# Group softmax on one core: GpSimdE instead of SyncE opens and closes the critical section and waits for the last two stores

## The chip, the cores and the metric

One core of a Trainium2 chip. The metric is the device time of one execution in microseconds (us). Durations of single instructions are in nanoseconds (ns). "The trace's records" are the start and duration of each single instruction in the trace; the views of the profile show them rounded to 0.1 us or summed up.

## The reference

```python
B, N, D, G = 4, 4096, 4352, 8          # x: float32, 285.2 MB; the output is as large
x_g = x.reshape(B, N, G, D // G)       # groups of 544 values
x_g = x_g - x_g.max(axis=-1, keepdims=True)
exp = np.exp(x_g)
out = exp / exp.sum(axis=-1, keepdims=True)
```

## The kernel before

The input is cut into 64 tiles of 128 partitions x 8704 values (4.4 MB), which pass through six buffers. SyncE issues the loads, VectorE takes each group's negative maximum, ScalarE the exponential with its sum, VectorE scales in place, and GpSimdE issues 62 of the 64 stores. SyncE issues the last two, since it has no loads left by then. The engines are ordered by semaphores alone, inside one critical section: one engine raises a flag that lets the others in, and at the end one engine raises a flag, collects the answers of the others, and all pass a final barrier.

```python
ctx.enter_context(tc.tile_critical(no_gpsimd_drain=True))   # SyncE opens and closes
...
for t in range(nt):                                          # SyncE: loads
    if t >= NT:
        nc.sync.wait_ge(stored[t % NT], 16 * (t // NT))
    ...
    nc.sync.dma_start(out=tile_in[:, :], in_=xt[t]).then_inc(landed[t % NT], 16)
    ...
for t in range(nt - LAST, nt):                               # SyncE: last two stores
    nc.sync.wait_ge(scaled, t + 1 if t < nt - 1 else len(parts))
    nc.sync.dma_start(out=ot[t], in_=bufs[t % NT][:, :]).then_inc(last_stored, 16)
nc.sync.wait_ge(last_stored, 16 * LAST)

for t in range(nt - LAST):                                   # GpSimdE: 62 stores
    nc.gpsimd.wait_ge(scaled, t + 1)
    nc.gpsimd.dma_start(out=ot[t], in_=bufs[t % NT][:, :]).then_inc(stored[t % NT], 16)
for t in range(nt - NT, nt - LAST):
    nc.gpsimd.wait_ge(stored[t % NT], 16 * (t // NT + 1))
nc.gpsimd.drain()
```

## Time and profile before

| | before |
|---|---|
| three runs | 1326.55, 1326.64, 1326.76 us |
| span of the profiled run | 1324.9 us |
| bytes moved | 570.5 MB at 431 GB/s over the span |
| first load issued | 0.960 us |
| sixteenth increment of the last store | 1323.532 us |
| from there to the end ("the tail") | 1.387 us |

The last three rows are from the trace's records. They cut the span in three: an opening without transfers, a stream of transfers that fills 99.8% of the time, and a tail without transfers. The lines of the profile that show it are in the prediction below.

### The profile page before, as it was taken

The numbers are of one execution on the slowest core, as the hardware profiler recorded it, in microseconds if no ns is written. First come the engines' busy times: TensorE is split into PE (matmuls) and PEld (weight loads), VectorE is DVE, ScalarE is ACT, GpSimd is POOL, SyncE is SP. The second block draws the span as 40 slices with busy tenths as digits, with TensorE's granted clock in tenths as the row PEclk, the third lists the DMA queues.
The fourth block names the chain that finished last, engine by engine and source line by source line (L and its number), as shares of the span: only waits on it lengthen the run. The fifth ranks groups of instructions, "written<-read, shape, count | busy, mean of one in ns | idle before, by whom it ended". The sixth has DMA issues, their size and how long they took to land.

```text
span 1324.9 us, 2463 instructions
## 1 busy us (share of the span) xinstructions
DVE 1190.0 (90%) x195; ACT 757.5 (57%) x2049; POOL 33.4 (3%) x66
## 2 busy tenths in 40 slices
DVE  5999999988989889898898998988989889898893
ACT  3765566547456465564655646556465474654751
POOL 0000000000000000000000000000000000000000
DMA  9999999999999999999999999999999999999998
GB/s 404 421 432 436 428 435 434 434 431 433 433 435 433 432 434 433 436 429 435 432 436 431 433 433 434 434 431 435 433 436 429 435 432 436 431 432 434 433 431 372
DMA packets 18582, 570.48 MB, mean 431 GB/s; under 512 B 2064, under 2 KB 2064, under 8 KB 2064
## 3 DMA queue, kind: packets, MB, share of 16 engines
q1 hardware_dynamic: 9648, 294.13, 51.5%
q0 software_dynamic: 8928, 276.30, 48.3%
q14 instruction: 6, 0.05, 0.0%
HBM read 285.21 MB, written 285.21 MB: 431 GB/s over the span
## 4 chain that ended last, share of the span: by engine, by line
another core or an unknown queue 69%; DVE 20%; DMA 7%; ACT 1%; SPq 1%; issue 0%
DVE xt L74 10%; DVE mx L61 10%; DMA out_dram<-xt 4%; DMA xt<-in_x_dram 4%; ACT xt L85 1%; SPq L104 1%; DVE rs L71 0%; SPq L166 0%; SPq L47 0%
## 5 line engine op out<-in xcount | busy, mean ns | idle before, releaser
L85 ACT ACTIVATE xt<-xt,mx 128x544 f32<-128x544 f32 x1024 | 750.2, 734 | 542.7 <-DVE mx L61 542.7
L61 DVE TENSOR_REDUCE mx<-xt 128x16 f32<-128x8704 f32 (+1 forms) x65 | 590.1, 9079 | 111.0 <-DMA xt<-in_x_dram 111.0
L74 DVE TENSOR_TENSOR xt<-xt,rs 128x8704 f32<-128x8704 f32 (+1 forms) x65 | 590.6, 9086 | 2.2
L85 ACT ACTIVATION_READ_ACCUMULATOR xt<-xt,mx 128x1 f32 x1024 | 191.8, 187 | 0.0
L118 POOL DMA_DIRECT2D out_dram<-xt x62 | 33.2, 535 | 1243.7 <-DVE xt L74 1243.7
L71 DVE RECIPROCAL rs<-sm 128x16 f32<-128x16 f32 (+1 forms) x65 | 15.7, 242 | 2.8 <-ACT xt L85 2.8
L123 ACT ACT_TABLE_LOAD x1 | 1.3, 1283 | 0.9 <-SPq L47 0.9
L155 POOL MEMSET const-float32-0.0<- 128x1 f32 x1 | 0.1, 99 | 0.2 <-issue 0.2
L155 POOL MEMSET const-bfloat16-1.0<- 128x1 bf16 x1 | 0.1, 102 | 0.0
L155 POOL MEMSET const-float32-1.0<- 128x1 f32 x1 | 0.1, 99 | 0.0
L155 POOL MEMSET const-uint8-127<- 128x1 uint8 x1 | 0.1, 99 | 0.0
## 6 DMA issues: line engine op xcount, KB each, us to landing
xt<-in_x_dram SPq DMA_DIRECT2D x63, 4352.0 KB, 33.1
out_dram<-xt POOLq DMA_DIRECT2D x62, 4352.0 KB, 50.6
out_dram<-xt SPq DMA_DIRECT2D x2, 4352.0 KB, 20.1
xt<-in_x_dram SPq DMA_DIRECT2D x2, 2176.0 KB, 36.0
```

The costliest lines, as they stand in the source:

```text
L61: i = nc.vector.reduce_max(out=mx[:, t % NT, g], in_=groups(t, g), axis=X, negate=True)
L71: nc.vector.reciprocal(out=rs[:, t % NT, g], in_=sm[:, t % NT, g]).wait_op(exp_done, n + 1, "sem-ge").then_inc(rec_done, 1)
L74: nc.vector.tensor_tensor(out=xg, in0=xg, in1=rs[:, t % NT, g].unsqueeze(2).to_broadcast([P, g.stop - g.start, Dg]), op=mybir.AluOpType.mu ...
L85: i = nc.scalar.activation(out=xg[:, g - gs.start, :], in_=xg[:, g - gs.start, :], func=Exp, bias=mx[:, t % NT, g:g + 1], scale=1.0, accum ...
L104: nc.sync.dma_start(out=tile_in[:, :], in_=xt[t]).then_inc(landed[t % NT], 16)
L118: nc.gpsimd.dma_start(out=ot[t], in_=bufs[t % NT][:, :]).then_inc(stored[t % NT], 16)
L123: nc.scalar.preload_act_table(Exp)
L155: nc = _bacc.Bacc("TRN2", target_bir_lowering=False, num_devices=1)
```

## The change

Its intent is to take one hand-over out of the two ends. GpSimdE releases the barrier at the start (at 0.646 us in the trace of the kernel before) and collects the one at the end (from 1324.168 us), so it may as well raise the section's flags, and SyncE can issue its first load without raising a flag first.

```diff
-    ctx.enter_context(tc.tile_critical(no_gpsimd_drain=True))
+    ctx.enter_context(tc.tile_critical(
+        sync_engine=mybir.EngineType.Pool, no_gpsimd_drain=True))
...
         nc.sync.dma_start(out=ot[t], in_=bufs[t % NT][:, :]).then_inc(last_stored, 16)
-    nc.sync.wait_ge(last_stored, 16 * LAST)
...
     nc.gpsimd.drain()
+    nc.gpsimd.wait_ge(last_stored, 16 * LAST)
```

## The prediction

What no trace or run of this case shows is cut from this text, and the cuts are marked. Where the text speaks of one DMA engine that ends behind the rest, what the trace has is one packet alone under way from 1321.769 to 1323.053 us, and the sixteenth increment 1.563 us after the fifteenth.

> **What bounds the kernel now.** I began with the head of the page, to see whether an engine is full.
>
> ```profile
> span 1324.9 us, 2463 instructions
> DVE 1190.0 (90%) x195; ACT 757.5 (57%) x2049; POOL 33.4 (3%) x66
> ...
> DMA  9999999999999999999999999999999999999998
> ...
> HBM read 285.21 MB, written 285.21 MB: 431 GB/s over the span
> ```
>
> VectorE is busy 90% of the time, but the DMA row is at nine tenths or more in 39 of 40 slices. Input and output are 4 x 4096 x 4352 values of four bytes, 285.2 MB each, so the 570.4 MB are what the problem demands, and at 431 GB/s they take 1324 us: the whole span. GpSimdE has 3% of work.
>
> Next the queue of SyncE, since the change takes duties from it.
>
> ```profile
> SPq L104 <- DMA out_dram<-xt: 1218.2, 58, 67.7
> SPq L112 <- DVE xt L74: 59.9, 2, 44.7
> ...
> SPq L155 <- PEq L155: 0.7, 1, 0.7
> SPq L166 <- SPq L166: 0.4, 1, 0.4
> SPq L166 <- PEq L166: 0.2, 1, 0.2
> ```
>
> Columns: microseconds waited in total, how many times, the longest. A load waits for the store that empties its buffer, 58 times, for 1218 us: one closed loop of transfers. The two lines that wait for VectorE are the final stores. All waits for other engines at the two ends of the program come to 0.7 + 0.4 + 0.2 us. That is the stuff the change rearranges.
>
> Then the stretches of the span, columns: length, busy time and instructions of each engine, clock, DMA share, GB/s.
>
> ```profile
> 1.00:100.00 99.00, 83.25 (x13) 57.52 (x154) 1.73 (x3) 1.00 0.99 422
> 100.00:1200.00 1100.00, 1008.15 (x164) 640.68 (x1736) 29.32 (x55) 1.00 1.00 433
> ...
> 1306.00:1323.60 17.60, 0.03 (x1) 0.00 (x0) 0.00 (x0) 1.00 0.81 350
> 1323.60:1324.90 1.30, 0.00 (x0) 0.00 (x0) 0.00 (x0) 1.00 0.00 0
> ```
>
> From 1.0 to 1323.6 us the transfers hold everything. Only the first 1.0 us and the last 1.3 us have no transfer in them. So 2.3 us, 0.17% of the span, is the most that any change to opening and closing could touch inside the span, and most of that stays.
>
> Last, what GpSimdE and SyncE do at the end, from the views of single lines (duration in ns, then start of the first and the last).
>
> ```profile
> L121 POOLq DRAIN  x1: 5129/5129/5129, 1312.1 to 1312.1; - x1
> ...
> L104 SPq COMPARE_BRANCH  x1: 33/33/33, 1323.5 to 1323.5; - x1
> ...
> L47 SPq EVENT_SEMAPHORE  x3: 17/17/28, 1323.7 to 1323.9; - x3
> ...
> L47 POOLq NOP  x1: 13/13/13, 1323.7 to 1323.7; - x1
> ```
>
> GpSimdE's own drain takes 5.13 us, but ends at 1312.08 + 5.13 = 1317.21 us. SyncE passes its wait for the last two stores only at 1323.55 us (the wait is carried by the branch that follows it). GpSimdE therefore stands idle for 6.3 us before the event that closes the section. This decides most of the question.
>
> [...] the last store's 16 increments come between 1320.31 and 1323.53 us, fifteen of them by 1321.97. Who waits for the sixteenth cannot make it come sooner. [...] The trace has 155 ns from SyncE's waiting branch at 1323.548, over one more branch, to its flag at 1323.703. [...] in the trace two successive semaphore instructions stand 78 ns apart on GpSimdE (1324.168 and 1324.246) and 64 to 70 ns on SyncE (1323.879, 1323.948, 1324.018, 1324.082), so they are close, with GpSimdE slightly slower.
>
> **The change, part by part.** I compared the two built programs, engine by engine. TensorE, VectorE and ScalarE keep every instruction; their flags merely come from GpSimdE. SyncE's loads and stores and GpSimdE's stores keep their order and waits. What moves is a handful of semaphore instructions: three fewer on SyncE, five more on GpSimdE.
>
> The opening. Before: GpSimdE leads the start barrier and releases it at 0.646 us; SyncE sees it (0.662), sets the section's flag (0.727, visible 0.743), and passes its own waiting branch at 0.803, 76 ns later than its flag instruction; the first load issues at 0.960, 157 ns after the branch. After: GpSimdE, which released the barrier with its instruction at 0.620, goes straight on to a branch and the flag, one step of 78 ns (estimate, from its spacing above): flag at about 0.70, visible at 0.72. SyncE, which no longer has a flag to set, reaches its branch where the flag instruction stood, about 0.727 to 0.74. The first load then issues about 157 ns later, at 0.89. Saved: 0.960 - 0.89 = 0.07 us. As the loads start a closed loop, this should move the whole schedule earlier by 0.07 us.
>
> The closing. Before, counted from the sixteenth increment at 1323.532: 16 ns to SyncE's branch, 155 ns to the flag (1323.703), then the answers of the others, three waits and a step, and SyncE's count into the final barrier at 1324.145; GpSimdE takes it up at 1324.168, 465 ns after the flag; from there to the end is 1324.919 - 1324.168 = 751 ns. After, GpSimdE has the same branch pair (16 + 155, estimate: same as SyncE). From its flag it needs: its own waiting no-op, 92 ns (SyncE's distance from flag to own answer, 1323.795 - 1323.703); two waits, a no-op and a branch with drain, 4 x 78 = 312; the drain's 34; and about 60 to the barrier's wait. Sum: 498 ns against 465, so 33 ns more. SyncE's chain runs beside it: its answer, two waits and two drains, one no-op fewer than before, about 465 - 64 = 401 ns. It hides behind the 498. The final barrier's 751 ns stay. Added: 0.03 us.
>
> GpSimdE's drain and its waits for older stores stay ahead of the new wait, and with 6.3 us of slack cost nothing. Sum: -0.07 + 0.03 = -0.04 us on 1326.64. I predict **1326.6 us**.
>
> **Rivals.** First, GpSimdE as closer is a slow one: if its drain and the wait ran one after the other, up to 5.1 us would be added, giving 1331.8 (0.4% slower). For it: the drain is the longest entry of all sequencer lines. Against it: the drain starts when an older store lands at 1311.97, not with the last one. It stays hidden unless that store lands over 6.3 us later.
>
> Second, the intended gain is real: SyncE saves a whole hand-over at the end because GpSimdE leads the final barrier. If the close collapsed to the barrier alone, the 613 ns from 1323.532 to SyncE's count at 1324.145 would shrink to perhaps 200, for 1326.2 us. Against it: SyncE still waits for all the answers before it enters the final barrier, so the trip is turned round rather than removed.
>
> Third, an early shift changes how loads and stores interleave. One of the 16 DMA engines ends 1.6 us behind the rest in the last store (1323.53 against 1321.97); an order that removed this would give 1325.0, and one that lengthened it by as much 1328.2. The loop's 58 waits, all of one kind, speak against a lasting effect of 0.07 us, yet this is the largest source of a difference over 0.2 us. [...]
>
> **Range and chances.** Three runs of before lie within 0.21 us (1326.55 to 1326.76), more than the effect I compute. The third rival sets the range: about two thirds of its 1.6 us either way gives 1325.5 to 1327.6. A change of 2% is 26.5 us, eleven times the 2.3 us without transfers, and neither drain nor stray engine reaches it. I give 0.99 to within 2%; the rest is for an effect on the stream of transfers that I do not see.
>
> **What would show it.** Right: first load issued at about 0.89 us; DMA share unchanged at 1.00 in the middle; the drain again about 5.1 us and over before the last store lands; GpSimdE's waiting branch within 20 ns of the last increment; 1.3 to 1.5 us from that increment to the end. Wrong: a drain that ends after the last store; a tail over 1.6 us or under 1.2; another spacing of the last store's increments; a middle that runs at another rate than 433 GB/s.

## The result, and the profile after

| | before | after |
|---|---|---|
| median, lowest to highest of 6 runs each | 1326.74 (1326.55 to 1327.48) | 1326.41 (1326.28 to 1326.50) |
| span of the profiled run | 1324.919 | 1324.654 |
| first load issued | 0.960 | 0.897 |
| first load to last increment | 1322.572 | 1322.368 |
| tail | 1.387 | 1.389 |

The ratio is 0.9997, with a 95% interval of 0.9984 to 1.001. Executions over 1.5% slower than the fastest of the same kernel are left out of the means.

The head of the page after the change:

```profile
span 1324.7 us, 2465 instructions
DVE 1190.0 (90%) x195; ACT 757.4 (57%) x2049; POOL 33.3 (3%) x66
...
HBM read 285.21 MB, written 285.21 MB: 431 GB/s over the span
```

There are two instructions more: the trace records six more on GpSimdE and four fewer on SyncE. Work and bandwidth are what they were. The waits of SyncE's queue after (total us, times, longest):

```profile
SPq L105 <- DMA out_dram<-xt: 1201.7, 57, 67.8
SPq L113 <- DVE xt L75: 59.1, 2, 43.9
SPq L108 <- DMA out_dram<-xt: 20.2, 1, 20.2
SPq L47 <- POOLq L47: 17.3, 1, 17.3
SPq L167 <- PEq L167: 0.8, 2, 0.5
SPq L156 <- PEq L156: 0.7, 1, 0.7
```

Against the lines before, the first group has lost one wait and 16.5 us (58 and 1218.2 before). This is not a gain: the lost wait was SyncE's for the last two stores, which stood in that group as it is carried by the branch of the same line (L104, at 1323.548 us). A wait of 17.3 us for GpSimdE's closing flag has come in its place. The wait moved, and it still ends when the last store lands.

The stretches after, cut where the transfers end (length, busy time and instructions of each engine, clock, DMA share, GB/s):

```profile
1.00:100.00 99.00, 83.31 (x13) 57.57 (x154) 1.73 (x3) 1.00 1.00 424
100.00:1200.00 1100.00, 1008.34 (x164) 640.58 (x1736) 29.23 (x55) 1.00 1.00 433
1306.00:1323.30 17.30, 0.00 (x0) 0.00 (x0) 0.00 (x0) 1.00 0.80 346
1323.30:1324.70 1.40, 0.00 (x0) 0.00 (x0) 0.00 (x0) 1.00 0.00 0
```

The middle runs at 433 GB/s as before, and 1.4 us without transfers remain at the end. The single lines at the close (durations in ns, then start of first and last):

```profile
L121 POOLq DRAIN  x1: 5129/5129/5129, 1311.8 to 1311.8; - x1
...
L105 POOLq COMPARE_BRANCH  x1: 33/33/33, 1323.3 to 1323.3; - x1
...
L47 POOLq EVENT_SEMAPHORE  x3: 17/17/43, 1323.4 to 1323.7; - x3
...
L47 SPq DRAIN  x1: 7/7/7, 1323.5 to 1323.5; - x1
```

The drain ends at 1311.80 + 5.13 = 1316.93 us, 6.3 us before the last increment at 1323.265. The waiting branch is now GpSimdE's (POOLq) and passes 24 ns after that increment.

So the profile pair shows 0.063 us gained in the opening, nothing in the tail (2 ns lost), and 0.204 us gained in the stream, in which the change touches no instruction. The prediction had the first two within 0.03 us. The experiments ask about the third, and about the rivals.

### The profile page after: what moved, and what is told of

Same layout as the page of the kernel before. It is cut to its first block, busy times and chain, and to the rows that moved or that the text cites. A ratio compares the mean times of both kernels' runs of the same rounds, so it can differ in the third digit from the quotient of the medians.

```text
span 1324.7 us, 2465 instructions
## 1 busy us (share of the span) xinstructions
DVE 1190.0 (90%) x195; ACT 757.4 (57%) x2049; POOL 33.3 (3%) x66
## 3 DMA queue, kind: packets, MB, share of 16 engines
q1 hardware_dynamic: 9648, 294.13, 51.5%
## 4 chain that ended last, share of the span: by engine, by line
another core or an unknown queue 69%; DVE 20%; DMA 7%; ACT 1%; SPq 1%; issue 0%; POOLq 0%
DVE xt L75 10%; DVE mx L62 10%; DMA out_dram<-xt 4%; DMA xt<-in_x_dram 3%; ACT xt L86 1%; SPq L105 1%; DVE rs L72 0%; SPq L167 0%; POOLq L47 0%; POOLq L156 0%
## 6 DMA issues: line engine op xcount, KB each, us to landing
out_dram<-xt POOLq DMA_DIRECT2D x62, 4352.0 KB, 51.5
out_dram<-xt SPq DMA_DIRECT2D x2, 4352.0 KB, 20.1
```

## The experiments

**First theory.** The change is worth about 0.06 us, all of it in the opening; the rest of the measured 0.3 us is wander of the stream of transfers, which differs from run to run of one program. **Rival one:** the stream is repeatable and the change moves it to a better order. **Rival two:** GpSimdE's drain is not really free. Twelve kernels ran, in three batches, each beside runs of the kernel before on the same chip. The batches ran on different chips, so a comparison across batches is weaker than one within a batch. All gave correct results.

### Both kernels once more

No edit; each program ran again.

> The kernel before, unchanged, against itself. First theory (the 0.3 us gain is 0.06 us of opening plus 0.2 us of wander in the stream of transfers): the medians agree within 0.2 us, the first load issues at 0.96 us, the tail from the last store's sixteenth increment to the end is 1.39 us, and against the earlier profile the stores in the middle of the span stand shifted by 0.1 to 0.5 us although the program is the same. Rival (the stream is repeatable and the change moves it): the two profiles of before agree within 0.1 us all along.

> The changed kernel, unchanged. Both theories: first load at 0.90 us, tail 1.39 us. First theory: median 0.06 us below the kernel before of the same rounds, give or take 0.2 us, so between 0.1 us slower and 0.3 us faster. Rival (the change moves the stream for good): 0.25 to 0.35 us below once more, with the same step of -0.35 us at 450 to 600 us in the middle of the span.

The kernel before: first load at 0.960 us and tail 1.387 us, to the nanosecond as in its first profile. Its stream took 1322.560 us. In the middle it did stray from its first profile: the stores of tiles 13 to 20 were issued 0.14 to 0.15 us later, those of tiles 25 to 31 some 0.1 us earlier, the last within 0.01 us. The part of the expectation on the times failed: six runs had a median of 1327.36 us against 1326.62 us (11 runs) for the same program beside it, as three of the six lay at 1328.0 to 1328.2 us. One program against itself differs by more than the whole result.

The changed kernel: first load 0.894 us, tail 1.389 us, stream 1322.506 us. The median was 1326.51 us, 0.11 us under the 1326.62 us beside it (ratio 1.0001, with one run of 1335.3 us in it). In its middle the stores of tiles 13 to 21 came 1.4 to 1.5 us later than in the first profile of the kernel before, while loads 6 to 15 were issued 1.5 to 1.7 us earlier; at the last stores the difference was -0.13 us. Rival one needed the same step of -0.35 us again. From tile 20 to tile 28 (432 to 597 us) the stores do fall back against that first profile, by 0.39 us after 0.34 us in the first pair. But the kernel before, run again, falls back by 0.25 us there too, and a later variant of the changed kernel (the one that drains last) by 0.05, so the step does not go with the change.

This is how the stream wanders: loads come earlier and stores later, or the reverse, by up to 1.7 us, and in these profiles the difference is returned by the end. From 1 to 1290 us the rate was 431 to 434 GB/s in every stretch of them that was looked at.

### Who raises the closing flag, and who waits

Two hybrids. In the first SyncE opens and closes as before, and only the wait for the last stores goes to GpSimdE:

```diff
-    nc.sync.wait_ge(last_stored, 16 * LAST)
...
     nc.gpsimd.drain()
+    nc.gpsimd.wait_ge(last_stored, 16 * LAST)
```

> SyncE opens and closes as before; only the wait for the last two stores is moved to GpSimdE. The closing flag then goes up 17 us early and ScalarE, VectorE and SyncE have answered by the time the last store lands. First theory: the tail shrinks from 1.39 us to about 1.12 us (16 + 148 ns to GpSimdE's answer, about 200 ns to SyncE's count, then the final barrier's 751 ns), the first load stays at 0.96 us, the time falls by 0.27 us against before. Rival (the close costs the final barrier alone whoever waits): the tail stays within 0.05 us of 1.39 us.

In the second GpSimdE opens and closes as in the changed kernel, but the wait stays with SyncE. It ran twice.

```diff
+        sync_engine=mybir.EngineType.Pool, no_gpsimd_drain=True))
...
     nc.sync.wait_ge(last_stored, 16 * LAST)
...
     nc.gpsimd.drain()
```

> GpSimdE opens and closes; the wait for the last two stores stays with SyncE. The closing flag goes up at about 1317.3 us, after GpSimdE's drain. First theory: first load at 0.90 us as in the changed kernel, tail about 1.24 us (16 + 155 ns to SyncE's answer, 286 ns through SyncE's waits, 32 ns, then 751 ns), time 0.06 + 0.15 = 0.21 us below before. Rival (closing costs the same whoever waits): tail 1.39 us.

> GpSimdE opens and closes, SyncE waits for the last stores: once more, since its first profile fell on a late last transfer. Tail 1.24 us again, first load 0.90 us, stretch from first load to last increment back at 1322.2 to 1322.7 us, lowest time 0.15 us below the changed kernel's 1326.28 if the tail passes to the time, otherwise within 0.1 us of it.

| kernel | first load | stream | tail | median (lowest) |
|---|---|---|---|---|
| SyncE flags, GpSimdE waits | 0.960 | 1322.371 | 1.273 | 1326.47 (1326.38) |
| GpSimdE flags, SyncE waits (five fast runs) | 0.898 | 1323.773 | 1.238 | 1326.40 (1326.30) |
| the same again | 0.895 | 1322.644 | 1.239 | 1326.55 (1326.38) |

The closing lines of the first hybrid, from the views of its single lines:

```profile
L47 SPq EVENT_SEMAPHORE  x3: 17/17/28, 1306.2 to 1306.5; - x3
...
L104 POOLq COMPARE_BRANCH  x1: 32/32/32, 1323.4 to 1323.4; - x1
...
L166 SPq DRAIN  x3: 7/7/130, 1323.6 to 1324.3; - x3
```

SyncE has its flag up and two of its waits done at 1306.5 us, 17 us before the last store lands. When GpSimdE's waiting branch passes, only GpSimdE's own answer is missing. From the last increment to the point where GpSimdE takes up the final barrier it is 375 ns, against 636 before (1324.168 - 1323.532); about 364 was expected (16 + 148 + about 200). But the tail is 1.273 us and not 1.12: the final barrier then took 898 ns instead of 751, since SyncE came late to its second half, with a pause of 440 ns between two instructions and a drain of 130 ns where others take 7. That pause returns below. Of the 0.27 us that were expected in the time, the medians show 0.15 (1326.47 against 1326.62).

The second hybrid gave its expected tail of 1.24 us twice. So the tail does get 0.11 to 0.15 us shorter where the flag goes up before the last store lands, and it gets no shorter where flag and wait merely move together. Rival "the close costs the same whoever waits" falls. The saving was not confirmed in the times. In its first batch the five fast runs had a median 0.22 us under the kernel before, where 0.21 was expected; in the second the medians were 1326.55 and 1326.56 us (kernel before), and the lowest, 1326.38, did not fall to 0.15 us below 1326.28. No version was shown to beat both kernels.

The first hybrid opens at 0.960 us like before, yet has a stream of 1322.371 us, within 3 ns of the changed kernel's first profile. That speaks for wander against rival one.

The stream of 1323.773 us is another thing. Time from issue to landing of the last two stores in that run, with its smallest, median and largest value:

```profile
DMA to landing us min/median/max: 18.8/21.6/24.3
```

In the profile before it was 17.5/20.1/22.8. From the trace's records: of 14 profiles, 12 have the last store land 17.46 to 17.53 us after its issue, and two 18.82 to 18.83 us after it. The 1.3 us between fit one packet: a 34,816-byte packet took 1.288 us (the median of either queue), as if one packet more had been to go at the end. In these two profiles it was long in coming: from tile 40 in one and tile 24 in the other the loads land 30.9 to 31.0 us after their issue, and most stores 53.2 us, where the first profile of the kernel before settles at 33.5 and 50.6. That is two packets' time each way (2 x 1.288 us). So a difference can also last, and in these two profiles the last store landed 1.3 us late. The two profiles belong to runs of 1327.68 and 1327.88 us. Runs between 1327.3 and 1328.2 us occur with the kernel before too (1327.48, 1327.50 and 1327.92 us among those it ran beside others); whether each had a late last packet was not seen, since only one run of each kernel is profiled.

### Is the drain free, and why

The changed kernel with the drain behind the wait, and the changed kernel without it:

```diff
-    nc.gpsimd.drain()
     nc.gpsimd.wait_ge(last_stored, 16 * LAST)
+    nc.gpsimd.drain()
```

> The changed kernel with two lines swapped: GpSimdE first waits for the last two stores, then drains. First theory (the drain is a fixed piece of work of 5.13 us that is free only because it runs while the last store is under way): the drain shows 5.13 us again, after the last increment, the tail grows from 1.39 to about 6.5 us and the time by 5.1 us to 1331.5 us. Rival (the drain lasts as long as software transfers are outstanding, and costs little once all has landed): drain well under 1 us, time within 0.5 us of the changed kernel.

```diff
-    nc.gpsimd.drain()
     nc.gpsimd.wait_ge(last_stored, 16 * LAST)
```

> The changed kernel without GpSimdE's own drain. First theory (the 5.13 us of work are done once, by the first drain after the stores): the first drain behind the closing flag takes the 5.1 us, now exposed, tail about 6.5 us, time about 1331.5 us. Rival (the work is tied to this one drain and vanishes with it): all remaining drains stay at 34 to 108 ns, tail 1.39 us, time as the changed kernel.

The line of the drain, first in the kernel that drains last, then the closing drains of GpSimdE in the kernel that has none of its own (smallest, median and largest of the three):

```profile
L122 POOLq DRAIN  x1: 5129/5129/5129, 1323.5 to 1323.5; - x1
```

```profile
L166 POOLq DRAIN  x3: 40/107/5129, 1323.8 to 1329.5; - x3
```

5129 ns each time, to the nanosecond, whether the drain begins before or after the last store lands, so it does not wait for that store. Whether its length depends on how many stores GpSimdE issued was not tested. GpSimdE's other drains take 34 to 181 ns in the first profiles of the kernels before and after. Taken out, the long one does not vanish: the first drain behind the closing flag, 34 ns in the changed kernel, does it instead, where nothing runs beside it. Tails: 6.486 and 6.577 us against 1.389. Medians: 1331.75 and 1331.60 us against 1326.82 for before in the same rounds (ratios 1.004 and 1.0037, intervals from 1.0020 up), as the first theory said: 1331.5. So the drain's place ahead of the wait, at a moment when GpSimdE has 6.3 us to spare, is worth 5 us (0.4%), about eighty times the 0.063 us that the change gains in the opening.

### What a later first load costs

If the stream is full from end to end, a late first load must come out at the end. SyncE got drains (about 52 ns each, as it turned out) ahead of its first load, in the changed kernel:

```diff
+    for _ in range(16):        # or 1, 8, 80
+        nc.sync.drain()
     for t in range(nt):
```

> The changed kernel with 16 SyncE drains of about 65 ns each ahead of the first load, some 1.05 us of delay. First theory (the transfers fill all the time from first load to last increment, so a shift of the start passes to the end one to one): first load at about 1.95 us, time 1.05 us longer give or take 0.3 us. Rival (the closed loop absorbs a shift of the start): the time stays within 0.3 us, and then the 0.06 us of the opening are worth nothing.

> The same with 80 drains, some 5.3 us of delay. First theory: first load at about 6.2 us, time 5.3 us longer give or take 0.4 us, stretch from first load to last increment 1322.4 to 1322.6 us as before. Rival: well under half of it reaches the end.

> The changed kernel with one SyncE drain ahead of the first load: the first load issues some 52 ns later, at 0.95 us, nearly where before has it (0.96), so the opening's gain is taken back. First theory (the opening's gain shifts the whole stream, but by less than the stream wanders by itself): tail 1.39 us, lowest time within 0.1 us of the lowest time of before, stretch from first load to last increment between 1322.2 and 1322.7 us. Rival (the change moves the stream to a better order, worth 0.2 us): this kernel loses it and stands 0.3 us above the changed kernel in lowest times, like before.

> Eight drains, some 0.42 us of delay, first load at 1.31 us. If a delay passes one to one: lowest time about 1326.7 us (1326.28 + 0.42). If a delay of the start costs about double, as 16 drains suggested in one profile (0.84 us of delay, 1.8 us at the end): about 1327.2 us.

> The 16 drains once more. If its extra 0.9 us came from late transfers by chance, the lowest of six runs is about 1327.1 us (1326.28 + 0.84) and some lie 1 us higher; if it belongs to the delay, all lie at 1328.0 us or more again.

| drains | first load later by | tail | profiled end later by | median, lowest (us) |
|---|---|---|---|---|
| 0 (changed kernel) | 0 | 1.389 | 0 | 1326.41, 1326.28 |
| 1 | 0.056 | 1.390 | 1.455 | 1326.67, 1326.35 |
| 8 | 0.421 | 1.647 | 0.596 | 1327.19, 1327.03 |
| 16 | 0.836 | 1.389 | 1.804 | 1328.65, 1328.02 |
| 16 again | 0.837 | 1.390 | 1.469 | 1328.06, 1327.90 |
| 80 | 4.606 | 1.389 | 7.044 | 1333.45, 1332.57 |

The differences are against the first profile of the changed kernel, which did not run again in these batches; the kernel before beside them had medians of 1326.82 us (16 and 80 drains) and 1326.56 us (1, 8 and 16 again). No delay was absorbed, so the rival falls. But with 16 and 80 drains more came out than went in, against the expectation, and the lowest time with 8 drains, 1327.03 us, lies between its two expectations (1326.7 and 1327.2). The repeat of the 16 shows that it is no chance: all nine runs of the 16 lie at 1327.9 us or more.

One drain puts the first load back to 0.953 us. Its lowest time, 1326.35 us, is 0.07 us over the changed kernel's lowest, and not the 0.3 us that rival one demands. This separates the two theories less than it seems, since the kernel before itself lay only 0.12 us over that time in this batch (1326.40). (Its profiled end is late by one last packet, 1.3 us, as above.)

The surplus with 16 drains has one place in the stream. VectorE's maxima are later by another 0.86 us (0.58 in the repeat) from tile 58 on, because the load of tile 58 landed late. Time from issue to landing in the first of the two profiles, of the loads issued from 1000 to 1130 us and then of tile 58's, issued at 1142.4 us:

```profile
DMA to landing us min/median/max: 33.2/33.3/33.4
...
DMA to landing us min/median/max: 34.4/34.4/34.4
```

The store of tile 54, under way at the same time, took 51.5 us (51.2 in the repeat), where the stores just before it took 50.6. Meanwhile the queue that the profile calls "instruction" moved two transfers of 8192 bytes, at 1168.98 and 1169.04 us (1168.91 and 1170.02 in the repeat). The other twelve profiles have one transfer near that time (1168.2 to 1175.1 us), and in none of them does tile 58's load take over 0.1 us longer than tile 57's. That queue from 1165 to 1172 us (packets, MB, share), with 16 drains and in the changed kernel:

```profile
q14 instruction: 2, 0.02, 0.6%
...
q14 instruction: 1, 0.01, 0.3%
```

That the second transfer makes the others late is not shown; it took 0.3 us itself, less than the delay. SyncE did not hesitate: tile 60's load, which needs the buffer of tile 54, came 21.49 us after the load before it (21.19 in the repeat) where 20.5 to 20.7 us is usual, but it was issued 16 ns after the increment that it waited for, as other loads are.

At other places SyncE does pause. Count the instructions of SyncE that the trace records, from 0: the pause is ahead of number 79, in all five profiles in which that one is not a waiting load. In the kernel before, in both profiles, it is in the final barrier: SyncE takes up its release 427 ns after its instruction before, at 1324.563 us, where ScalarE does at 1324.292. GpSimdE is clearing semaphores meanwhile (160 ns, from 1324.463 us), and the barrier takes 751 ns, as in the changed kernel, which has no such pause; so it costs nothing. In the hybrid with SyncE's flag it is the 440 ns pause in the barrier; it costs 0.15 us there. With 8 drains it falls between SyncE's answer and its next wait, 423 ns instead of 85, and the tail is 1.647 us:

```profile
L47 SPq DRAIN  x1: 7/7/7, 1323.8 to 1323.8; - x1
...
L169 SPq EVENT_SEMAPHORE  x4: 17/17/28, 1324.2 to 1325.2; - x4
```

With 80 drains number 79 is a drain; it came 392 ns after its predecessor (the ones before it 45 to 57) and took 133 ns. The first load, four instructions on, took 1.83 us to issue where it takes 0.38 in the other kernels; the largest of the three durations in ns:

```profile
L107 SPq DMA_DIRECT2D xt<-in_x_dram x63: 327/328/1834, 5.5 to 1231.0; - x63
```

In each of these five profiles a transfer of 8192 bytes starts on the instruction queue 0.63 to 0.65 us after number 79 starts (with 80 drains at 5.80 us). In the seven profiles where SyncE has only 78 or 79 recorded instructions, the changed kernel's among them, no such pause shows, and that transfer comes 1.0 to 1.1 us after the end of the span. With 16 drains number 79 is tile 60's load, which waits for its buffer anyway; the second transfer at 1169 to 1170 us seems to be the same one, as none follows later.

With the pause the 8 drains add up: against the kernel before of the same batch, the first load is 0.36 us later and the tail 0.26 us longer, 0.62 of the 0.63 us between the medians. The 16 add up with the late landings: 0.84 and 0.58 to 0.86 are 1.42 to 1.70, with 1.47 and 1.80 in the profiles. Of the 80's 7.04 us, 6.06 are explained (the second load is late by that much: about 4.2 us for 80 drains of 52 ns and, as an estimate, the remaining 1.9 for the pause and the slow first load); the remaining 1.0 us comes in gradually between tiles 13 and 57, and its cause is open. What the pause is was not shown: no run forced it by itself, and the transfer on the instruction queue starts after it, so the transfer is not what the pause waited for.

## Why the prediction was right

**The bound.** Right: 433 GB/s in the middle before and after, and a delay of the first load is not absorbed (with the first load 0.421 us later the profiled end is 0.596 us later, with 4.606 it is 7.044).

**The opening, -0.07 us.** Right, by its own mechanism: the first load moved from 0.960 to 0.897 us, -0.063. GpSimdE's flag came at 0.700 (0.70 predicted), SyncE's branch at 0.739 (0.727 to 0.74), the load 158 ns later (157). In the first pair the stores of the first 13 tiles were each issued 67 ns earlier, as the prediction had it for the whole schedule; then the wander sets in.

**The closing, +0.03 us.** It was +0.002, so the 0.03 us were not added. The step that was mis-sized is the chain from GpSimdE's flag to the final barrier: 498 ns predicted, 1323.903 - 1323.437 = 466 measured, against 465 before. The 78 ns that I took for each step are GpSimdE's spacing in the barrier. In the closing chain the five steps took 100, 93, 60, 87 and 48 ns, and 78 to the barrier. The branch came 24 ns after the increment and not within the 20 that the prediction named as a sign, the branch pair, from the waiting branch to the flag, took 148 ns (155), and the final barrier 751 ns as before. Two readings were off without harm. Of the 58 waits that the prediction puts down to loads, one was for the last two stores. And the wait of 0.4 us "SPq L166 <- SPq L166" is no wait for another engine but SyncE's pause of 427 ns ahead of its instruction 79. The kernel before has that pause where it costs nothing, and the changed kernel, with 78 recorded instructions on SyncE, ends before it, so nothing was gained or lost.

**The drain.** Right that it costs nothing in this order. The first rival's 5.1 us are real, as the two drain experiments show, but only for an order that the change does not use.

**The hand-over.** The second rival said that collapsing the close would save time. The changed kernel does not collapse it, as predicted: flag and wait move together, so the flag still goes up after the last store. Two hybrids that part them did save 0.11 and 0.15 us of tail.

**The size.** Predicted -0.04 us, measured -0.33 between the medians of the first batch and -0.11 in the second. Opening and tail explain 0.06. The other 0.2 us of the first profile pair are in the stream. That they are wander is argued from its spread: it is 1322.27 to 1322.64 us in all eight profiles without added delay or late last packet (those of the two drain experiments among them), with either opening. The six runs of after lay under all six of before in the first batch; later runs of before came down to 1326.38 us and overlap them. A small lasting part of the 0.2 us cannot be excluded by these runs; nothing needs it. The third rival had this as the largest source of difference, and the range of 1325.5 to 1327.6 us held the median. One thing that the prediction named as a sign of being wrong did occur: the last store's sixteenth increment came 0.755 us after its fifteenth, and not 1.563 as before. The sign says little, as the gap is 0.857 us in the second profile of the kernel before, and the store took 17.5 us from issue to landing in all three. So the two ends were right by their mechanism. The total was held by a range some fifty times as wide as the computed effect, and that the measured gain was larger than 0.04 us was not foreseen.

## What to carry to other kernels

When the transfers fill the span, read off first how many microseconds at either end have none: that is the ceiling of what any change to opening and closing can gain there, here 2.3 us, of which 0.06 were got. It can lose more: the drain behind the last store cost 5 us. At the close, let the flag and the slow drain (5129 ns) come before the last transfer lands, so that only one answer is missing when it does; here the early flag took 0.11 to 0.15 us from the tail, which the times did not confirm. Judge effects under 1 us by instructions in the trace and by repeats of both kernels, since one program's median moved by 0.7 us against itself.
